# A layer of two mixers on one core: three result buffers for the convolutions, X loaded into the inversion's own tiles, v turned one block later, and two groups of gate columns moved

## The chip, the core and the metric

The kernel runs on one core of a Trainium2 chip. The metric is the device time of one execution in microseconds, and lower is better. The core has a matrix engine (TensorE, in the profile PE, with its weight loads as PEld), VectorE (DVE), ScalarE (ACT), GpSimd (POOL) and SyncE (SP), which here only issues transfers. They run their own instruction streams in order and wait for each other by semaphores. ScalarE and GpSimd issue transfers too.

## The reference

One layer of a diffusion backbone works on 1024 latent tokens and 256 context tokens of width 1024, in float32:

```
h = modulate(rms_norm(x), shift, scale)          # for latent and for context tokens
p = h @ w_in                                     # one projection for both groups of heads
q, k, v = silu(short_conv(p[:, :1536]))          # 4 heads of 128 each
A = tril(k_beta k^T * decay, -1);  T = (I + A)^-1    # one triangular inverse per chunk, head and direction
o_gdn = gated delta rule, both directions        # a scan over chunks; then * silu(z)
o_ret = retention, both directions               # rq and rk with rotary angles; then * silu(rg)
x = x + g1 * (concat(o_gdn, o_ret) @ w_out)
x = x + g2 * swiglu(modulate(rms_norm(x)))
out = rms_norm(x, final_g)
```

The reference scans in chunks of 64 tokens. The kernel uses chunks of 128: 10 in all, 2 of context and 8 latent.

## The kernel before

All of build is written out in Python and scheduled at build time: a planner runs a model of the engines over the program and lays down one fixed order for each engine. Among the instructions that it takes to be ready it picks the one that stands first in the program, so later work fills the holes of earlier work. The order on the chip is then fixed, also where the chip's times differ from the model's.

Memory: pools are stacked from the left or the right side of the on-chip memory. A pool opened after another has been closed lies on the same bytes, and a tile of it waits until the tiles that lay there have been read for the last time. A tag with bufs=n has n slots in turn.

The steps around the change, in the order of the program:

- k blocks, then q blocks. conv_block(b, y, lat) multiplies 128 columns of w_in with all tokens (72 matmuls of three-part float32 products; 48 for q, which needs only latent tokens), copies the two or three chunks from the pc banks of PSUM (2) to u and, scaled, to y with ScalarE (lines 608 and 609), adds four shifted products with VectorE (615), and applies Silu with ScalarE (618). The tiles y come from newy() and have 2 slots, u has 2. Behind each q block qstat turns the q of the block before and sums squares (686, 688), with the pb banks (3).
- token_major(g, ...) multiplies the tokens, tile by tile of 128, with a group of 256 columns: two weight halves, each split in two parts by ScalarE (344) and VectorE or GpSimd (345) into the slots of pool W (2 each; W2 for early groups), then 24 matmuls for a token tile (371 to 373) into a pa bank (3 banks). Groups 0 and 1 are rv, 2 and 3 rk, 4 and 5 rq, 6 and 7 rg (the gate of the retention), 8 and 9 z (the gate of the other group of heads). The finishing step is a Silu (fin_gate, 532) or the rotary turn (fin_rope, 524 to 529, with a scratch tile ra in pool R1). Before the change groups 6 and 7 stand behind the q blocks, groups 8 and 9 behind merge 2, and rk and rq behind the first two steps of the scan.
- solve(b) for the chunks of BATCH 0 (0, 1, 2, 9) and BATCH 1 (3, 8, 4, 7): pre(t) makes the matrices of a chunk. It loads k and q of the chunk (659) and rows of decays (gw, 737), multiplies (729, 734), masks (741, GpSimd), exponentiates (745) and writes U (748) and sp (750). invert(b) sends the diagonal blocks of 32 by 32 to DRAM (yd, 766), loads them back one block to a partition (yr, 768), copies them to L (774, and turned 775), sets X to the identity with GpSimd (771, 772), runs 31 pairs of updates on VectorE (781, 783), and stores X and its turned copy XT (785, 787).
- v blocks. Behind each one its y is turned right away, with ten transposes into three pa banks (871), three copies to vt (873, 2 slots) and three stores issued by ScalarE (874). Then pool CV (y, u, vt) is closed.
- Pools RP (the rope table, loaded by line 887) and GM (matrices U of BATCH 2, t64, xt) open on the bytes of CV. pre(2), merge(0), invert(2), merge(1) and merge(2) follow. A merge loads the inverted blocks (802, 803) and joins them to blocks of 64 and then of 128, with small matmuls (822, 829, 832, 845, 849), copies scaled by -1 on VectorE (825, 846) and copies on ScalarE (835, 838, 851), and stores U (853).
- GM is closed, SC and PK open on its bytes, and the scan over the chunks begins (steps, lines 917 and on).

Of the kernel before, what the change touches and what calls it, by code (L numbers as in the profile page):

```python
# [8 lines left out]
F32 = mybir.dt.float32  # L9
F32R = mybir.dt.float32r  # L10
I32 = mybir.dt.int32
AF = mybir.ActivationFunctionType
ALU = mybir.AluOpType
# [4 lines left out]
P = 128  # L18
# [20 lines left out]
def build(nc, tc, ap, dbg=None, stop=None, marks=None):  # L39
# [19 lines left out]
    def close(p):  # L59
        p_close.pop(id(p)).close()  # L60
# [130 lines left out]
    try:  # L191
# [197 lines left out]
        def token_major(g, tiles, finish, store, pl, q=S):  # L389

            w = [tm_weights(g, kh, pl, q) for kh in range(2)]

            for p in range(0, len(tiles), 2):
                pair = [(t, tm_bank(g)) for t in tiles[p:p + 2]]
                for kh in range(2):
                    for t, o in pair:
                        tm_half(o, w[kh], kh, t)
                for t, o in pair:
                    tm_store(g, t, o, finish, store, pl)
# [118 lines left out]

        def fin_rope(t, o, res):
            cos, sin = rope[:, t, 0:64], rope[:, t, 64:128]  # L520
            ra = R1.tile([P, 2, 2, 64], F32, tag="ra", name="ra")
            o4 = o.rearrange("p (h a d) -> p h a d", a=2, d=64)
            r4 = res.rearrange("p (h a d) -> p h a d", a=2, d=64)
            V.tensor_tensor(ra.rearrange("p h a d -> p (h a) d"), o.rearrange("p (g d) -> p g d", d=64),
                            bc(cos, [P, 4, 64], 1), ALU.mult)
            for a in range(2):
                V.tensor_tensor(r4[:, :, a, :], o4[:, :, 1 - a, :], bc(sin, [P, 2, 64], 1), ALU.mult)
            for a, op in ((0, ALU.subtract), (1, ALU.add)):
                G.tensor_tensor(r4[:, :, a, :], ra[:, :, a, :], r4[:, :, a, :], op)
# [88 lines left out]
            S.activation(y[:, a0:], y[:, a0:], AF.Silu)  # L618

        def newy():  # L620
            return CV.tile([P, NTOK], F32, tag="y", name="y", bufs=2)

        a4, b4, kds4, neG4 = (sm[n].rearrange("p (t d h) -> p t d h", d=2, h=4) for n in ("ab", "beta", "kds", "neG"))

# [39 lines left out]
        V.tensor_scalar(sm["g"], sm["neG"], -1.0, None, ALU.mult)  # L664
        V.tensor_scalar(nkf, nkf, EPS, None, ALU.add)

        lnk = log(GS, nkf, TT * H, "ln").rearrange("p (t h) -> p t h", h=H)
        nG4 = sm["nG"].rearrange("p (t d h) -> p t d h", d=2, h=H)
        V.tensor_scalar(lnk, lnk, 0.5, None, ALU.mult)
        Gr = R2.tile([P, TT, 2, H], F32, tag="Gr", name="Gr", bufs=1)  # L670
# [32 lines left out]
        checkpoint("q")  # L703
        token_major(6, LAT, fin_gate, S, W2, SY)
        qstat(H - 1, qys[H - 1])
        token_major(7, LAT, fin_gate, S, W2, SY)
        checkpoint("rg")
        close(R2)
        close(W2)
# [48 lines left out]
        def invert(b):  # L758

            nc_ = len(BATCH[b])  # L760
            nu = nc_ * H
            nb = 4 * nu
            xd = xds[b] = dr.tile([4 * nb, 1024], F32, tag="xd%d" % b, name="xd%d" % b)
            yr = GI.tile([P, 1024], F32, tag="yr", name="yr", bufs=1)
            for k in range(4):
                SY.dma_start(yd[b][:, k].rearrange("u i j -> i u j"),
                             us[b][q32[k]].rearrange("p e c h j -> p (e c h) j")[:, :, q32[k]])
            SY.dma_start(yr[:2 * nb], yd[b].rearrange("u k i j -> (u k) (i j)"))
            L = GI.tile([P, 1024], F32, tag="L", name="L", bufs=2)
            X = GI.tile([P, 1024], F32, tag="X", name="X", bufs=1)  # L770
            G.memset(X, 0.0)
            G.memset(X[:, 0::33], 1.0)
            m = lambda t: t[:2 * nb].rearrange("p (i j) -> p i j", j=32)
            S.activation(L[:nb], yr[:nb], AF.Copy)
            V.tensor_copy(m(L)[nb:], yr[nb:2 * nb].rearrange("p (i j) -> p j i", j=32))
            for j in range(31):
                n = 31 - j
                tmp = GI.tile([P, 256], F32, tag="tmp", name="tmp", bufs=1)
                t3 = tmp[:2 * nb, :n * (j + 1)].rearrange("p (i c) -> p i c", c=j + 1)
                sh = [2 * nb, n, j + 1]  # L780
                V.tensor_tensor(t3, bc(m(L)[:, j + 1:, j], sh, 2), bc(m(X)[:, j, :j + 1], sh, 1), ALU.mult)
                xs = m(X)[:, j + 1:, :j + 1]
                V.tensor_tensor(xs, xs, t3, ALU.subtract)
            XT = GI.tile([P, 1024], F32, tag="L", name="XT", bufs=2)
            V.tensor_copy(m(XT), X[:2 * nb].rearrange("p (i j) -> p j i", j=32))
            for i, x in enumerate((X[:nb], XT[nb:2 * nb], X[nb:2 * nb], XT[:nb])):
                SY.dma_start(xd[i * nb:(i + 1) * nb], x)
# [19 lines left out]
        def merge(b):  # L807

            uu, ub, t64 = blocks(b)
            nu = len(BATCH[b]) * H  # L810
            q = q32
            u = [x.rearrange("p c h j -> p (c h) j") for x in ub]
            t = t64


            pairs = [(d, p) + ((2 * p, 2 * p + 1) if d == 0 else (2 * p + 1, 2 * p)) for p in range(2) for d in range(2)]
            three = lambda ps, sl, w: ps[sl].rearrange("p (n j) -> p n j", j=w)
            ps1 = bank_b("m1")
            for n in range(nu):
                for d, p, a, bb in pairs:  # L820
                    ca = (a % 2) * 32
                    T.matmul(ps1[q[bb], n * 32:n * 32 + 32], u[d][q[a], n, q[bb]], t[d][q[a], n, ca:ca + 32],
                             start=True, stop=True)
            xt1 = GM.tile([P, 16, 32], F32, tag="xt", name="xt1", bufs=1)
            V.tensor_scalar(xt1.rearrange("p n j -> p (n j)")[:, :nu * 32], ps1[:, :nu * 32], -1.0, None, ALU.mult)
            ps2, ps3 = bank_b("m1"), bank_b("m1")
            for n in range(nu):
                for d, p, a, bb in pairs:
                    T.matmul(ps2[q[a], n * 32:n * 32 + 32], xt1[q[bb], n, :], u[d][q[bb], n, q[bb]],
                             start=True, stop=True)  # L830
                    if p == d:
                        T.matmul(ps3[q[bb], n * 32:n * 32 + 32], u[d][q[bb], n, q[bb]], xt1[q[bb], n, :],
                                 start=True, stop=True)
            for d, p, a, bb in pairs:
                S.activation(u[d][q[a], :, q[bb]], three(ps2[:, :nu * 32], q[a], 32), AF.Copy)
                if p == d:
                    ca = (a % 2) * 32
                    S.activation(t[d][q[bb], :, ca:ca + 32], three(ps3[:, :nu * 32], q[bb], 32), AF.Copy)
            halves = [(0, slice(0, 64), slice(64, 128)), (1, slice(64, 128), slice(0, 64))]
            for n0 in range(0, nu, 8):  # L840
                ps1, ps2 = bank_b("m2"), bank_b("m2")
                xt2 = GM.tile([P, 8, 64], F32, tag="xt", name="xt2", bufs=1)
                for n in range(8):
                    for d, A, B in halves:
                        T.matmul(ps1[B, n * 64:n * 64 + 64], u[d][A, n0 + n, B], t[d][A, n0 + n, :], start=True, stop=True)
                V.tensor_scalar(xt2.rearrange("p n j -> p (n j)"), ps1, -1.0, None, ALU.mult)
                for n in range(8):
                    for d, A, B in halves:
                        T.matmul(ps2[A, n * 64:n * 64 + 64], xt2[B, n, :], u[d][B, n0 + n, B], start=True, stop=True)
                for d, A, B in halves:  # L850
                    S.activation(u[d][A, n0:n0 + 8, B], three(ps2, A, 64), AF.Copy)
            for c, t in enumerate(BATCH[b]):
                S.dma_start(sd[t, :, 1:8:6], uu[:, :, c].rearrange("p e h j -> p e (h j)"))
            checkpoint("mrg%d" % b)
# [5 lines left out]
            invert(b)  # L860
            checkpoint("inv%d" % b)

        solve(0)
        solve(1)
        for h in range(H):
            y = newy()
            conv_block(8 + h, y, False)
            for t0, n in ((0, 2), (2, 4), (6, 4)):
                ps = bank_a("vT")
                for t in range(t0, t0 + n):  # L870
                    T.transpose(ps[:, (t - t0) * P:(t - t0 + 1) * P], y[:, t * P:(t + 1) * P], ident)
                vt = CV.tile([P, 4, P], F32, tag="vt", name="vt", bufs=2)
                S.activation(vt[:, :n], ps[:, :n * P].rearrange("p (t j) -> p t j", j=P), AF.Copy)
                S.dma_start(vd[t0:t0 + n, :, h, :].rearrange("t p j -> p t j"), vt[:, :n])
        close(CV)
        checkpoint("v")
        RP = pool("rp", side="right")
# [13 lines left out]
        merge(2)  # L891


        for g in (8, 9):
            token_major(g, LAT, fin_gate, S, W)
        checkpoint("rgz")
        close(GM)
        close(G2)
# [1 line left out]
        close(GU)  # L900


        SC = pool("sc", bufs=2, side="right")
        PK = pool("pk", side="right")
        dy = dr.tile([LT, P, D], F32, tag="dy", name="dy")
# [247 lines left out]
        close(RT)  # L1153
        close(PK)
        close(SC)
        close(RP)
        close(GS)

# [518 lines left out]
```

## Time and profile before

| | us |
|---|---|
| median of 3 runs (lowest, highest) | 1490.18 (1489.36, 1492.62) |
| time of the profiled execution | 1488.32 |
| its span | 1486.5 |
| granted TensorE clock in it, mean | 0.977 |

The profiled execution's span is 1.8 us shorter than its time, and its time is 1.9 us below the median of the runs. Busy time is given for each engine; "idle before, releaser" tells what ended the idle time in front of an instruction. A line number is that of the kernel before. In a row of the timeline come start, duration, engine, line, operation, output<-inputs, shape and count. The group tm is the work of token_major, b that of conv_block, m that of merge.

### The profile page before, as it was taken

Reading aid. Unit: us, or ns where it says so; the run is one execution under the profiler, and the core shown is the slowest. Engines: PE = TensorE matmul, PEld = TensorE weight load, DVE = VectorE, ACT = ScalarE, POOL = GpSimd, SP = SyncE. Lnnn points to the kernel's source line nnn. Section 1 sums busy time; section 2 is a strip of 40 time slices with the busy share of each in tenths; the row PEclk is TensorE's granted clock in tenths of the full one; section 3 lists DMA queues with packets and bytes.
Section 4 is the critical chain, followed back from the end, with each engine's and each line's share of the span. In section 5 each row is a group of like instructions: output and inputs, shape, how many; then the busy total and the mean of one; then the engine's idle time right before and its main releaser. Section 6 shows DMA issues by size and latency. Waiting matters only on the chain. (4 is left out here: it accounts for less than half of the span.)

```text
span 1486.5 us, 24142 instructions
## 1 busy us (share of the span) xinstructions
PE 1407.3 (95%) x8919; PEld 1207.9 (81%) x8919; DVE 978.0 (66%) x1909; ACT 618.0 (42%) x1342; POOL 579.6 (39%) x493
## 2 busy tenths in 40 slices
PE   7999999996988999899799899999999999999997
PEld 2798888875978999889688688877888888788886
DVE  6568786568666335789777786656555554658577
ACT  5543553866331111346544533323333333444445
POOL 0130010221102344245235588899555553335321
PEclk9999999999889999999899999999999999999999
DMA  9536676478745743996633265765222242685863
GB/s 334 187 105 232 179 235 194 137 221 227 178 130 136 288 165 115 412 367 192 223 124 114 85 210 212 256 236 191 107 107 106 106 145 73 224 293 184 299 220 114
DMA packets 167766, 284.78 MB, mean 192 GB/s; under 512 B 43208, under 2 KB 93592, under 8 KB 163936
## 3 DMA queue, kind: packets, MB, share of 16 engines
q1 hardware_dynamic: 116096, 239.80, 47.6%
q10 hardware_dynamic: 49072, 35.83, 7.8%
q0 software_dynamic: 2480, 7.60, 1.4%
q8 instruction: 70, 1.15, 0.3%
q14 instruction: 48, 0.39, 0.1%
HBM read 201.36 MB, written 81.84 MB: 191 GB/s over the span
## 5 line engine op out<-in xcount | busy, mean ns | idle before, releaser
L371 PE MATMUL tm<-whi,hhi 128*128 128x256 f32 (+1 forms) x704 | 202.7, 293 | 7.5 <-ACT whi L344 3.0
L372 PE MATMUL tm<-wlo,hhi 128*128 128x256 f32 (+1 forms) x704 | 202.8, 290 | 0.7 <-DVE wlo L345 0.7
L373 PE MATMUL tm<-whi,hlo 128*128 128x256 f32 (+1 forms) x704 | 201.4, 290 | 0.0
L371 PEld LDWEIGHTS tm<-whi,hhi 128*128 128x128 f32 x704 | 136.0, 195 | 10.7 <-ACT whi L344 3.2
L372 PEld LDWEIGHTS tm<-wlo,hhi 128*128 128x128 f32 x704 | 137.2, 195 | 2.7 <-DVE wlo L345 1.2
L1366 PE MATMUL ffn<-t,wlo 128*128 128x512 f32 x352 | 137.1, 390 | 1.6 <-DVE wlo L345 1.6
L1364 PE MATMUL ffn<-t,whi 128*128 128x512 f32 x352 | 137.0, 390 | 1.4 <-ACT whi L344 1.4
L373 PEld LDWEIGHTS tm<-whi,hlo 128*128 128x128 f32 x704 | 136.3, 195 | 1.6 <-issue 0.9
L1365 PE MATMUL ffn<-t,whi 128*128 128x512 f32 x352 | 137.0, 389 | 0.0
L344 ACT ACTIVATE whi<-wraw 128x512 fp32r<-128x512 f32 (+2 forms) x98 | 75.2, 771 | 133.1 <-PE ffn L1365 80.2
L344 ACT ACTIVATE whi<-ws 128x512 fp32r<-128x512 f32 x88 | 55.6, 632 | 173.8 <-PE ffn L1365 121.0
L345 DVE TENSOR_TENSOR wlo<-ws,whi 128x512 fp32r<-128x512 f32 x88 | 94.7, 1078 | 48.4 <-ACT whi L344 48.2
L1490 PE MATMUL fo<-whi,ahi 128*128 128x512 f32 x308 | 119.3, 389 | 1.0 <-ACT ahi L344 1.0
L1491 PE MATMUL fo<-wlo,ahi 128*128 128x512 f32 x308 | 119.9, 389 | 0.0
L1492 PE MATMUL fo<-whi,alo 128*128 128x512 f32 x308 | 119.0, 390 | 0.0
L345 DVE TENSOR_TENSOR wlo<-wraw,whi 128x512 fp32r<-128x512 f32 (+2 forms) x92 | 101.5, 1105 | 19.5 <-ACT whi L344 19.2
L1364 PE MATMUL ffn<-b,whi 128*128 128x512 f32 x264 | 103.9, 394 | 5.1 <-ACT whi L344 5.1
L1366 PE MATMUL ffn<-b,wlo 128*128 128x512 f32 x264 | 103.6, 392 | 0.7 <-DVE wlo L345 0.7
L1365 PE MATMUL ffn<-b,whi 128*128 128x512 f32 x264 | 103.4, 392 | 0.0
L615 DVE SCALAR_TENSOR_TENSOR y<-u,cw,y 128x1022 f32<-128x1022 f32 (+3 forms) x80 | 81.9, 1040 | 19.7 <-ACT y L609 19.2
L607 PE MATMUL b<-hhi,wlo 128*128 128x512 f32 (+1 forms) x256 | 94.7, 370 | 0.0
L606 PE MATMUL b<-hlo,whi 128*128 128x512 f32 (+1 forms) x256 | 94.3, 368 | 0.0
(451 smaller groups left out, 3440.1 us busy)
## 6 DMA issues: line engine op xcount, KB each, us to landing
adaw<-ada SPq DMA_DIRECT2D x48, 512.0 KB, 4.4
pk<-sd SPq DMA_DIRECT2D x16, 1536.0 KB, 15.0
wraw<-wfi SPq DMA_DIRECT2D x44, 512.0 KB, 4.2
ar<-ad SPq DMA_DIRECT2D x33, 512.0 KB, 4.2
w<-wfo SPq DMA_DIRECT2D x22, 512.0 KB, 4.3
wd<-tw SPq DMA_DIRECT2D x11, 1024.0 KB, 4.9
ad<-act SPq DMA_DIRECT2D x20, 512.0 KB, 3.1
raw<-wd SPq DMA_DIRECT2D x20, 512.0 KB, 4.7
```

Source lines behind the costliest of these rows:

```text
L344: S.activation(hi, raw, AF.Copy)
L345: e.tensor_tensor(lo, raw, hi.bitcast(F32), ALU.subtract)
L371: T.matmul(o, hhi[:, k, tsl], whi[:, k % 4, :], start=(k == 0), stop=False)
L372: T.matmul(o, hhi[:, k, tsl], wlo[:, k % 4, :], start=False, stop=False)
L373: T.matmul(o, hlo[:, k, tsl], whi[:, k % 4, :], start=False, stop=(k == KT - 1))
L607: T.matmul(o, wlo[:, k, :], hh, start=False, stop=(k == KT - 1))
L1364: T.matmul(o, whi[:, k, :], xhi(xn, slice(0, 4), k), start=(first and k == 0), stop=False, **kw)
L1365: T.matmul(o, whi[:, k, :], xlo(xn, slice(0, 4), k), start=False, stop=False, **kw)
L1366: T.matmul(o, wlo[:, k, :], xhi(xn, slice(0, 4), k), start=False, stop=(k == 3), **kw)
L1490: T.matmul(po[g][i], ahi[:, ts], whi, start=(j == 0 and not kw), stop=False, **kw)
L1491: T.matmul(po[g][i], ahi[:, ts], wlo, start=False, stop=False, **kw)
L1492: T.matmul(po[g][i], alo[:, ts], whi, start=False, stop=(j == FH - 1), **kw)
```

## The change

- y has 3 slots in place of 2 (newy).
- token_major(7), the second half of rg, moves from behind the q blocks to behind the last v block. token_major(8), the first half of z, moves from behind merge(2) to the same place. Both now use pool W.
- v is turned by a function vturn, called for block h-1 behind block h, and for the last block behind groups 7 and 8. vt shrinks to two tiles of 128, so a block is copied and stored in five pieces (was three).
- In invert the loaded rows go straight to X[nb:2nb] and L[:nb]; yr and ScalarE's copy go. X has 2 slots (was 1) and is set to the identity by VectorE, behind the turned copy that reads it. XT is L itself, no longer a second slot.
- In merge the two copies scaled by -1 move from VectorE to ScalarE.
- The scratch ra of fin_rope moves from R1 to a pool RA that opens when GM has been closed, ahead of SC. The scratch of log moves from GS to R2.

```diff
-            ra = R1.tile([P, 2, 2, 64], F32, tag="ra", name="ra")
+            ra = RA.tile([P, 2, 2, 64], F32, tag="ra", name="ra")
...
-            return CV.tile([P, NTOK], F32, tag="y", name="y", bufs=2)
+            return CV.tile([P, NTOK], F32, tag="y", name="y", bufs=3)
...
-        lnk = log(GS, nkf, TT * H, "ln").rearrange("p (t h) -> p t h", h=H)
+        lnk = log(R2, nkf, TT * H, "ln").rearrange("p (t h) -> p t h", h=H)
...
         token_major(6, LAT, fin_gate, S, W2, SY)
         qstat(H - 1, qys[H - 1])
-        token_major(7, LAT, fin_gate, S, W2, SY)
...
-            yr = GI.tile([P, 1024], F32, tag="yr", name="yr", bufs=1)
+            L = GI.tile([P, 1024], F32, tag="L", name="L", bufs=2)
+            X = GI.tile([P, 1024], F32, tag="X", name="X", bufs=2)
...
-            SY.dma_start(yr[:2 * nb], yd[b].rearrange("u k i j -> (u k) (i j)"))
-            L = GI.tile([P, 1024], F32, tag="L", name="L", bufs=2)
-            X = GI.tile([P, 1024], F32, tag="X", name="X", bufs=1)
-            G.memset(X, 0.0)
-            G.memset(X[:, 0::33], 1.0)
+            rows = yd[b].rearrange("u k i j -> (u k) (i j)")
+            SY.dma_start(X[nb:2 * nb], rows[nb:])
+            SY.dma_start(L[:nb], rows[:nb])
...
-            S.activation(L[:nb], yr[:nb], AF.Copy)
-            V.tensor_copy(m(L)[nb:], yr[nb:2 * nb].rearrange("p (i j) -> p j i", j=32))
+            V.tensor_copy(m(L)[nb:], X[nb:2 * nb].rearrange("p (i j) -> p j i", j=32))
+            V.memset(X, 0.0)
+            V.memset(X[:, 0::33], 1.0)
...
-            XT = GI.tile([P, 1024], F32, tag="L", name="XT", bufs=2)
+            XT = L
...
-            V.tensor_scalar(xt1.rearrange("p n j -> p (n j)")[:, :nu * 32], ps1[:, :nu * 32], -1.0, None, ALU.mult)
+            S.activation(xt1.rearrange("p n j -> p (n j)")[:, :nu * 32], ps1[:, :nu * 32], AF.Copy, scale=-1.0)
...
-                V.tensor_scalar(xt2.rearrange("p n j -> p (n j)"), ps1, -1.0, None, ALU.mult)
+                S.activation(xt2.rearrange("p n j -> p (n j)"), ps1, AF.Copy, scale=-1.0)
...
+        def vturn(h, y):
...
+                for t in range(t0, t0 + n, 2):
+                    vt = CV.tile([P, 2, P], F32, tag="vt", name="vt", bufs=2)
+                    S.activation(vt, ps[:, (t - t0) * P:(t - t0 + 2) * P].rearrange("p (t j) -> p t j", j=P), AF.Copy)
+                    S.dma_start(vd[t:t + 2, :, h, :].rearrange("t p j -> p t j"), vt)
...
+        vys = []
         for h in range(H):
-            y = newy()
-            conv_block(8 + h, y, False)
...
+            vys.append(newy())
+            conv_block(8 + h, vys[h], False)
+            if h:
+                vturn(h - 1, vys[h - 1])
+        token_major(7, LAT, fin_gate, S, W)
+        token_major(8, LAT, fin_gate, S, W)
+        vturn(H - 1, vys[H - 1])
         close(CV)
...
-        for g in (8, 9):
-            token_major(g, LAT, fin_gate, S, W)
+        token_major(9, LAT, fin_gate, S, W)
...
+        RA = pool("ra", bufs=2, side="right")
         SC = pool("sc", bufs=2, side="right")
...
         close(SC)
+        close(RA)
```

More of the change, by code (lines that the diff above doesn't have):

```diff
@@ L861, in solve @@
             checkpoint("inv%d" % b)
-        solve(0)
-        solve(1)
-        for h in range(H):
-            y = newy()
-            conv_block(8 + h, y, False)
+        def vturn(h, y):
             for t0, n in ((0, 2), (2, 4), (6, 4)):
@@ L871, in build @@
                     T.transpose(ps[:, (t - t0) * P:(t - t0 + 1) * P], y[:, t * P:(t + 1) * P], ident)
-                vt = CV.tile([P, 4, P], F32, tag="vt", name="vt", bufs=2)
-                S.activation(vt[:, :n], ps[:, :n * P].rearrange("p (t j) -> p t j", j=P), AF.Copy)
-                S.dma_start(vd[t0:t0 + n, :, h, :].rearrange("t p j -> p t j"), vt[:, :n])
+                for t in range(t0, t0 + n, 2):
+                    vt = CV.tile([P, 2, P], F32, tag="vt", name="vt", bufs=2)
+                    S.activation(vt, ps[:, (t - t0) * P:(t - t0 + 2) * P].rearrange("p (t j) -> p t j", j=P), AF.Copy)
+                    S.dma_start(vd[t:t + 2, :, h, :].rearrange("t p j -> p t j"), vt)
+        solve(0)
+        solve(1)
+        vys = []
+        for h in range(H):
+            vys.append(newy())
[5 more added lines that the diff above has]
+        vturn(H - 1, vys[H - 1])
         close(CV)
```

## The prediction

> **What bounds the kernel now.** I read the page first (engines, slices, granted clock), then busy time by stage, then what TensorE waits for, then the rows around the edited lines.
>
> ```profile
> span 1486.5 us, 24142 instructions
> PE 1407.3 (95%) x8919; PEld 1207.9 (81%) x8919; DVE 978.0 (66%) x1909; ACT 618.0 (42%) x1342; POOL 579.6 (39%) x493
> PEclk9999999999889999999899999999999999999999
> ```
>
> TensorE is busy for 95% of the span, so what it idles or runs slowly is what can be won. Each digit of the clock is a fortieth of the span, 37 us: two 8 stand side by side from 372 to 446 us. By stage (columns: length, busy time and count of PE, PEld, DVE, ACT, POOL, granted clock, DMA share, GB/s):
>
> ```profile
> 236.00:262.00 26.00, 26.00 (x207) 23.90 (x205) 14.25 (x41) 9.77 (x32) 1.11 (x2) 1.00 0.66 195
> 290.00:371.00 81.00, 64.62 (x389) 56.48 (x387) 62.53 (x96) 55.10 (x120) 15.34 (x17) 0.95 0.79 228
> 371.00:398.00 27.00, 26.60 (x202) 26.40 (x202) 17.07 (x45) 10.27 (x19) 5.32 (x5) 0.89 0.62 163
> 398.00:439.00 41.00, 36.72 (x640) 34.62 (x640) 29.74 (x77) 10.42 (x19) 2.71 (x3) 0.88 0.52 131
> 439.00:500.00 61.00, 53.46 (x959) 50.28 (x960) 33.13 (x86) 13.76 (x24) 16.75 (x30) 0.92 0.68 202
> 500.00:583.00 83.00, 83.00 (x712) 83.00 (x712) 33.62 (x110) 9.79 (x19) 36.17 (x74) 1.00 0.41 150
> ```
>
> TensorE's largest waits from 236 to 500 (total, times, longest):
>
> ```profile
> PE vT L871 <- ACT y L618: 11.2, 3, 8.7
> PE kq L734 <- issue: 5.2, 2, 2.6
> ```
>
> From 290 to 500 TensorE idles for 16.4 + 0.4 + 4.3 + 7.5 = 28.6 us, 11.2 of them ahead of the turns of v. Behind a stall it also runs slowly (last columns: clock, DMA, GB/s):
>
> ```profile
> 372.00:376.00 4.00, 4.00 (x20) 0.50 0.42 123
> 444.00:448.00 4.00, 4.00 (x21) 0.50 1.10 202
> ```
>
> The missing clock times the length of each stage gives 4.1 + 3.0 + 4.9 + 4.9 = 17 us; part of it falls into idle time, so I count 14. Some 42 us are thus lost from 290 to 500, and no more can be won. From 500 to 583 TensorE is full at full clock, so I pass a shift made ahead of 500 on to the end one to one.
>
> **The change, part by part.** *The third buffer of y, and group 7 taken out of the q stage.*
>
> ```profile
> 230.76 0.60 ACT L608 ACTIVATE u<-b 128x512 f32<-128x512 f32 x1 [3.34 <-PE b L607]
> 260.09 1.26 ACT L609 ACTIVATE y<-b,cw 128x512 f32<-128x512 f32 x2
> L371 PE MATMUL tm<-whi,hhi x63: 279/281/365, 236.1 to 261.5; 128*128 128x256 f32 x63
> 262.66 0.39 PE L605 MATMUL b<-hhi,whi 128*128 128x512 f32 x1
> ```
>
> The copy of q2 to y comes 29 us after that to u: it waits for a slot of y. The last q block cannot start until 262.66, and group 7 (64 triples, 63 of them in this row) fills TensorE meanwhile: 26.00 busy of 26.00. With three slots the q block runs at 236 and group 7 later; TensorE does the same work in another order, so I price this at 0. What covers it: the q and v blocks themselves. If that fails, nothing fills in any more; the two kq waits of 2.6 us are the nearest rows, so 0 to +6, and no gain of its own. The solves start some 22 us sooner, and VectorE, busy for only 14 of 26 us here and for 62.5 of 81 in the v stage, gets its work spread out.
>
> *v turned one block later.*
>
> ```profile
> 369.76 1.27 ACT L618 ACTIVATE y<-y 128x1280 f32<-128x1280 f32 x1 [0.49 <-DVE y L615]
> 371.08 2.40 PE L871 MATMUL vT<-ident,y 128*128 128x128 f32 x10 [8.73 <-ACT y L618]
> ```
>
> TensorE stands before the last turn because VectorE finishes the convolution late, with an inversion interleaved. In the new order another block, and at the end groups 7 and 8, lie between, so the 11.2 us and the half clock behind 371 (2 us in 372:376, 3 in all) go. Late next: the first tiles of group 7, since the turns of v2 hold all three pa banks until ScalarE has copied them, now in five pieces of two tiles through two slots.
>
> ```profile
> DMA to landing us min/median/max: 1.8/4.1/4.7
>   DMA sd<-vt: 5.2, 3
> ```
>
> (Both of tile vt: time to landing, and ScalarE's idle time until a slot's store has landed.) A piece through a slot costs a copy, an issue and 1.8 us at the least; three waits for a block where there was one. I take 4 us of TensorE at the start of group 7 (0 to 8); what is queued behind on ScalarE are the conv copies, which have the slack of two pc banks.
>
> *Groups 7 and 8 ahead of the last turn.* A group is 192 matmuls; the step between starts is
>
> ```profile
> 424.44 0.28 PE L373 MATMUL tm<-whi,hlo 128*128 128x256 f32 x1
> 427.50 0.28 PE L372 MATMUL tm<-wlo,hhi 128*128 128x256 f32 x1
> 399.00 0.22 PE L822 MATMUL m<-t,U 32*32 32x32 f32 x2 [1.32 <-DMA t<-xd]
> 441.85 1.01 PE L371 MATMUL tm<-whi,hhi 128*128 128x256 f32 x3 [3.03 <-ACT whi L344]
> ```
>
> 3.06 us over 26 steps = 0.118, so a group is 22.6 us. Between groups the two weight slots turn over: the two lower rows are the boundaries 8 to 9 and 9 to rk. The new boundary 7 to 8 costs 1.3 to 6 us (3.03 and as much again at half clock); I take 4.5.
>
> [...]
>
> *Sum up to the end of group 8.* Before, that point is 397.5, with 16.8 idle and, of the 7.1 of clock, about 4 outside it lost since 290: 21. After, lost: the kq waits 5.2 and 1.6 of clock, 4 at the start of group 7, 4.5 at the boundary: 15.3. Gain **6 us**: group 8 ends near 391.5, and the last turn of v comes behind it, as the program orders it.
>
> *Behind the last turn: pre(2), inversion 2, merge 2.* Matrices 2 and t64 lie where CV's y was, so this chain begins at the last turn (373.5 before, 391.5 after). The rope's scratch ra, until now in R1, is put where the merges' xt lies: no rope before merge 2 has read it.
>
> ```profile
> L524 DVE TENSOR_TENSOR ra<-tm,rope x10: 406/418/425, 451.1 to 492.6; 128x256 f32<-128x256 f32 x10
> L371 PE MATMUL tm<-whi,hhi x93: 276/281/579, 441.8 to 497.2; 128*128 128x256 f32 x93
> 497.63 1.15 PE L849 MATMUL m<-U,xt 64*64 64x64 f32 x32
> ```
>
> Before, 93 triples of rk (32.8 us) filled TensorE during merges 1 and 2. After, only three tiles fit (three pa banks, 8.5 us), and 24.3 us move behind merge 2. The length of the chain, from these rows:
>
> ```profile
> 377.88 0.33 SPq L887 DMA_DIRECT2D rope<-rope  x1
> 378.31 0.38 SPq L737 DMA_DIRECT2D gw<-grow_d  x1
> 385.12 0.69 DVE L748 TENSOR_TENSOR U<-kk,gw 128x512 f32<-128x512 f32 x1 [3.56 <-ACT gw L745]
> 311.79 1.60 SPq L766 DMA_DIRECT2D yd<-U  x3
> 329.77 1.39 DVE L775 COPY L<-yr 64x1024 f32<-64x1024 f32 x1
> 395.56 0.21 DVE L781 TENSOR_TENSOR tmp<-L,X 128x31 f32<-128x31 f32 x1 [5.13 <-POOL X L772]
> 428.44 1.06 DVE L785 COPY XT<-X 128x1024 f32<-128x1024 f32 x1
> 433.87 0.20 DVE L781 TENSOR_TENSOR tmp<-L,X 64x31 f32<-64x31 f32 x1 [2.52 <-POOL X L772]
> 469.43 0.78 SPq L787 DMA_DIRECT2D xd<-X  x2
> 480.71 0.24 PE L822 MATMUL m<-t,U 32*32 32x32 f32 x2 [2.29 <-DMA t<-xd]
> 433.00:470.00 37.00, 22.28 (x63) 0.91 0.57 151
> ```
>
> (The last row is VectorE on tile X alone.) Last turn to U: 385.8 - 373.5 = 12.3. U to the loaded block: 18.0 in batch 0 (311.8 to 329.8), with other loads in the queue; 9 if only issues and landings count; I take 10, the queue being emptier. The turned copy and two memsets now on VectorE: 2. The updates: 22.3 busy, 35.5 with rope and weights between; those are gone, so 24. Stores and reloads 469.4 to 480.7: 11.3. Merge 2: 18 (480.7 to 498.8) with matmuls of rk between; without them I take 13. Sum **73 us**; ends 66 (with 9, 1, 22.3 and 10) and 97 (with 18, 2, 35.5 and 18). TensorE's work within it: group 9 22.6, merges about 25 (101 less 22.6, 32.8, 12 idle and 9 of clock), rk 8.5: 56. It idles for 17.
>
> Before, 398 to 499 held the same work and 24.3 us more of rk: 101. After: 73 + 24.3 + 1.7 (half clock at the restart) = 99. Gain **2 us**.
>
> *The small ones together.* Direct loads into L and X, X double and zeroed on VectorE, XT in L: the waits for X ahead of L781, 5.13 and 2.52, go; 5.13 is inversion 1's, hidden by groups 7 and 8, and 2.52 lies ahead of my 24. xt on ScalarE in place of VectorE: a copy for a copy, in a merge with slack. lnk in R2: nothing. Each is priced at nothing; uncovered, the two waits would be a gain of 7.6. If inversions 0 and 1 were still running at 391, their 33 us each (395.6 to 428.4, with two weights between) would lengthen the chain; starting 22 us sooner, they should end near 380.
>
> Sum: 6 + 2 = 8 us. The profiled execution took 1488.3 us (span 1486.5): 1480.3. The median of the three runs stands 1.9 above it: **1482 us**.
>
> **The rivals.** (1) *The last turn slips ahead of group 8.* If the planner sees a hole in TensorE at the boundary 7 to 8, the ten turns go there, and the chain starts 22.6 us sooner, over 56 + 22.6 = 79 us of work, longer than the chain. Of the 17 idle us some 4 stay, for the next boundary of groups. Gain 6 + 2 + 13 = 21, time 1469. For it: merge 0's pair at 399.00 stands exactly at such a boundary. Against: that pair is ahead of the group in the program, the turn is behind it.
>
> (2) *Slower: rk waits for merge 2.* The chain grows as its pieces did before (18, 35.5, 18): 97 us, 22 more than 101 - 24.3 - 1.7 = 75 allows. The rope table's load waits for the last vt store, and gw behind it on SP, which gives it 4 more us easily. With the 6 it turns slower from a chain of 81 us; at 97 the time is 1506, typically (88) 1497. For it: slow pieces are what the trace shows. Against: their neighbours on VectorE are gone.
>
> (3) *No change.* The q and v blocks wait uncovered for y, u or pb, as the kq rows do, for 6 to 10 us, and the 8 are gone: 1490.
>
> **How the numbers follow.** Forecast 0.42, rival 1 0.25, rival 2 0.20, rival 3 0.13. The forecast's own range, chain 68 to 80: 1477 to 1489. 0.2% (3 us) is about what tells a change from none here. Faster: 0.33 of the forecast and 0.25 = 0.58. Same: 0.06 and 0.08 of rival 3 = 0.14. Slower: 0.03, 0.20, 0.05 = 0.28. The range leaves out the far ends of rivals 1 and 2: 1465 to 1500.
>
> **What would show it.** Right: no group of rows tm between the q blocks at 236 to 262; vT no longer waits for y; a gap of TensorE of some 17 us behind group 9; the first ra row only behind the last L849 row. Rival 1: vT between the matmuls of group 7 or 8. Rival 2: from last vT to the last merge over 81 us. The prediction fails if ra lands on free memory, or if inversion 1 still runs when pre(2) is done.

## The result and the profile after

The changed kernel takes **1505.8 us** (median of 4 runs, 1503.1 to 1510.1); the kernel before, run beside it, 1489.8 us. The ratio is 1.0109, 95% interval 1.0080 to 1.0139: **16 us slower**, where 1482 was predicted. The profiled execution took 1506.0 us, its span 1504.2. All medians here and below are of fast runs; one run, of e9, was slow (2839.7 us) and is left out.

The page of the changed kernel, the same three lines as before:

```profile
span 1504.2 us, 24164 instructions
PE 1399.9 (93%) x8919; PEld 1202.0 (80%) x8919; DVE 976.6 (65%) x1907; ACT 618.5 (41%) x1353; POOL 577.8 (38%) x487
PEclk9999999999995899999899999999999999999999
```

As many matmuls, TensorE 93% busy instead of 95%, and in the slice from 451 to 489 us a 5, where the kernel before has no digit under 8. The stages (columns as in the prediction):

```profile
236.00:262.00 26.00, 16.38 (x97) 12.49 (x95) 15.93 (x40) 8.39 (x28) 2.40 (x1) 0.87 0.59 176
262.00:351.00 89.00, 79.47 (x472) 68.80 (x470) 61.20 (x92) 66.93 (x184) 21.11 (x21) 0.98 0.71 204
351.00:400.00 49.00, 48.70 (x399) 48.65 (x400) 40.48 (x93) 13.70 (x28) 0.00 (x0) 0.97 0.47 135
400.00:450.00 50.00, 42.04 (x687) 39.78 (x687) 26.56 (x66) 17.78 (x33) 3.34 (x3) 0.97 0.72 169
450.00:485.00 35.00, 21.32 (x712) 19.30 (x713) 12.46 (x39) 13.08 (x25) 0.84 (x3) 0.56 0.70 224
485.00:610.00 125.00, 115.12 (x972) 114.73 (x972) 48.16 (x152) 13.00 (x24) 52.35 (x106) 0.96 0.41 150
```

Two stages that were full are not any more: the q stage (16.38 busy of 26) and the tm stretch behind the merges (115 of 125). In 450 to 485 TensorE is busy for 21 of 35 us, at a clock of 0.56. The stages of v and of groups 7 and 8, 262 to 400, are in order. Whom TensorE waits for, from 200 us to the first ffn matmul (total, times, longest; rows in order of time):

```profile
PE gr L504 <- DVE acc L499: 8.7, 1, 8.7
...
PE tm L371 <- ACT vt L870: 3.3, 2, 2.8
PE vT L867 <- ACT y L618: 2.1, 1, 2.1
...
PE m L844 <- ACT t L837: 5.2, 5, 1.8
PE m L828 <- ACT xt L824: 4.2, 2, 2.5
PE m L848 <- ACT xt L845: 4.1, 4, 1.4
...
PE kS L939 <- DVE S L967: 9.8, 1, 9.8
...
PE ro L1114 <- DMA vg<-rd: 11.9, 1, 11.9
```

The waits for y ahead of the turns are down from 11.2 to 2.1 us. New are 8.7 us in the q stage, some 14 in the merges' round trips to ScalarE, 9.8 at the scan's second step, and 11.9 late in the retention. Where the kernels stand at four points, by the end or start of TensorE's rows in each trace (us; e2 and e4 are explained below):

| | before | changed | e2 | e4 |
|---|---|---|---|---|
| last turn of v ends | 373.5 | 400.5 | 401.5 | 374.7 |
| last merge ends | 498.8 | 483.3 | 497.4 | 489.8 |
| tm matmuls left then | 588 | 792 | 557 | 792 |
| last tm ends | 582.9 | 608.4 | 579.3 | 603.9 |
| first ffn matmul | 838.8 | 857.3 | 831.5 | 854.6 |

The changed kernel is 15.5 us ahead when the merges end, and 25.5 behind when tm ends.

### The profile page after: what moved, and what is told of

Its sections match the earlier page's. It is cut to its first block, busy times and chain, and to the rows that moved or that the text cites. A ratio compares the mean times of both kernels' runs of the same rounds, so it can differ in the third digit from the quotient of the medians.

```text
span 1504.2 us, 24164 instructions
## 1 busy us (share of the span) xinstructions
PE 1399.9 (93%) x8919; PEld 1202.0 (80%) x8919; DVE 976.6 (65%) x1907; ACT 618.5 (41%) x1353; POOL 577.8 (38%) x487
## 4 chain that ended last, share of the span: by engine, by line
PE 52%; DMA 8%; DVE 8%; POOL 6%; issue 3%; ACT 2%; SPq 2%; ACTq 0%; POOLq 0%; DVEq 0%
PE ffn L1376 6%; PE ffn L1374 6%; PE ffn L1375 6%; PE fo L1500 5%; PE fo L1502 5%; PE fo L1501 5%; PE tm L373 3%; PE tm L371 3%; PE tm L372 3%; PE op L1235 2%; PE op L1233 2%; PE op L1234 2%; DMA gw<-grow_d 2%; DMA wd<-tw 2%; DMA sd<-U 1%
## 5 line engine op out<-in xcount | busy, mean ns | idle before, releaser
L371 PE MATMUL tm<-whi,hhi 128*128 128x256 f32 (+1 forms) x704 | 199.0, 287 | 6.3 <-ACT vt L870 3.3
L373 PE MATMUL tm<-whi,hlo 128*128 128x256 f32 (+1 forms) x704 | 198.1, 285 | 0.0
L372 PEld LDWEIGHTS tm<-wlo,hhi 128*128 128x128 f32 x704 | 133.9, 190 | 2.6 <-DVE wlo L345 1.2
L605 PE MATMUL b<-hhi,whi 128*128 128x512 f32 (+1 forms) x256 | 95.0, 371 | 2.0 <-ACT y L609 2.0
## 6 DMA issues: line engine op xcount, KB each, us to landing
pk<-sd SPq DMA_DIRECT2D x16, 1536.0 KB, 11.9
```

Of the source, the lines that this page charges most:

```text
L371: T.matmul(o, hhi[:, k, tsl], whi[:, k % 4, :], start=(k == 0), stop=False)
L372: T.matmul(o, hhi[:, k, tsl], wlo[:, k % 4, :], start=False, stop=False)
L373: T.matmul(o, hlo[:, k, tsl], whi[:, k % 4, :], start=False, stop=(k == KT - 1))
```

## The experiments

The theory (A in the expectations): the loss consists of holes that each belong to one part, the late place of ra above all. Its rival: the chain behind the last turn bounds, whatever lies beside it.

**e1, the q stage's hole.**

```diff
 conv_block(h, y, True)
-if h < 2:
-    ada_rest(5, h)
 ...
 if h:
     qstat(h - 1, qys[h - 1])
+if h < 2:
+    ada_rest(5, h)
```

> The changed kernel with one reordering: in the q stage the turns of the q block before (qstat) stand ahead of the second pair of coefficient rows (ada_rest(5, .)) instead of behind them. Theory A (the loss is made of holes, each belonging to one part): TensorE stands 8.7 us at 248 because the coefficient matmul L504, which waits for its weights, stands ahead of the turns that free the y slot the next v block needs; with the turns first the hole goes and the kernel is 8 to 13 us faster than the changed one, about 1495. Rival (the chain behind the last turn of v is all that bounds): the v blocks start earlier but wait for VectorE or a y slot later, and the time stays within 3 us of 1506.

Measured: 1498.5 us (10 runs, 1488 to 1501), ratio to the kernel before 1.0049 (1.0027 to 1.0071): 7 us faster than the changed kernel. Its q stage has one wait of 2.5 us left, and the last turn ends at 393.5 instead of 400.5. So the hole was real, and its cause the order on TensorE; the gain is just under the 8 to 13 us that theory A expected.

**e2, ra early; e3, both; e4, ra late in the kernel before.** e2 in the changed kernel:

```diff
-ra = RA.tile([P, 2, 2, 64], F32, tag="ra", name="ra")
+ra = RP.tile([P, 2, 2, 64], F32, tag="ra", name="ra", bufs=2)
 ...
-RA = pool("ra", bufs=2, side="right")
```

RP, the rope's pool, opens behind the last turn of v. e3 is e1 and e2 together. e4 is the kernel before with the changed kernel's two ra lines.

> The changed kernel with ra taken from the rope's pool, which opens behind the last turn of v, instead of a pool opened behind merge 2: the rope of rk can run during the merges again. Theory A: the merges' 13.7 us of holes and half clock from 450 to 485 are filled, and so is the 9.8 us hole at 493, where the scan's second step stands with no rk beside it: 10 to 25 us faster than the changed kernel, 1481 to 1496, with well over 80 tm matmul triples of rk before the last merge. Rival (the merge chain bounds, whatever fills it): the chain from the last turn to the last merge grows by as much as rk brings forward, gain under 4 us.

> Both edits of e1 and e2 in the changed kernel. Theory A: the two gains add, 18 to 35 us faster than the changed kernel, 1471 to 1488, so at or below the kernel before. Rival (one bound behind both): no better than the better of e1 and e2 by more than 3 us.

> The kernel before with nothing changed but ra's place: from a pool that opens behind merge 2. Theory A: taking rk out of the merges alone costs 12 to 25 us, 1502 to 1515, with the tm matmuls of rk limited to three tiles before the last merge. The prediction's reckoning (the chain shortens once rk's rows leave VectorE, which pays for the 24.3 us of rk that move behind it): within 7 us of 1490.

Measured: e2 **1481.7 us**, ratio 0.9943 (0.9921 to 0.9965); e3 1480.1, ratio 0.9928 (0.9908 to 0.9948); e4 **1504.8**, ratio 1.0107 (1.0054 to 1.0159). ra's place alone decides the sign. It costs 24 us in the changed kernel and 15.5 in the kernel before (1489.3 in these runs), about as much as the whole change loses; the rest of the change gains 8. e4's four runs scatter (1499.5 to 1515.1), so by its interval its cost lies anywhere from 8 to 24 us; that it is less than in the changed kernel is not clear from the times. The stretch of the merges, and the first rope, changed kernel first and then e2:

```profile
483.45 0.42 DVE L524 TENSOR_TENSOR ra<-tm,rope 128x256 f32<-128x256 f32 x1 [21.51 <-PE m L848]
```

```profile
441.22 0.42 DVE L524 TENSOR_TENSOR ra<-tm,rope 128x256 f32<-128x256 f32 x1 [0.35 <-PE tm L373]
419.00:497.40 78.40, 71.02 (x1502) 67.17 (x1503) 41.34 (x108) 27.28 (x48) 20.24 (x37) 0.96 0.70 191
L371 PE MATMUL tm<-whi,hhi x81: 274/281/582, 445.8 to 496.0; 128*128 128x256 f32 x81
```

In the changed kernel the first rope waits for the last merge, 21.51 us with VectorE idle. In e2 it runs at 441; by the last merge 103 triples of rk are done, 81 of them from 445.8 on (third row), against 24 in the changed kernel, and TensorE is busy for 71 of 78 us at 0.96. e2's merges end 14 us later with 235 fewer tm matmuls to go (792 - 557; 27.7 us at the prediction's 0.118). e3's time lies in theory A's wide range too, but it is not the sum (7 and 24 us off 1505.8 would be 1475), and the rival, at most 3 us better than e2, fits: its last turn is 7 us sooner than e2's and its tm ends 6.9 sooner (572.4), but its first ffn matmul only 2.0 sooner (829.5), and the time 1.6, within the scatter. The scan and the retention give it back; which wait there takes it was not traced to one row. e1's 7 us are so a gain only while ra is late.

**e5, the rope table's load moved.** In the changed kernel the last piece of vt leaves its bytes so late (its store, issued at 408.16, lands 1.8 us later) that the table's load, and the gw load behind it on SP, go out 10 us behind the last turn (410.06 and 410.51, against 400.5). The edit, and the same in e3 as e6:

```diff
-SY.dma_start(rope, ap["rope"])
 invert(2)
+with tc.issue_after(loaded[0]):    # behind inversion 2's load of L
+    SY.dma_start(rope, ap["rope"])
```

> The changed kernel with the load of the rope table moved behind inversion 2's loads on SP. In the changed kernel the last gw load (410.51) stands on SP behind the rope load (410.06), which waits until the last of the five vt pieces has left the bytes that the table takes; from the last turn to inversion 2's stores 22.6 us pass, against 12.3 before. Theory A: with gw ahead that piece falls to about 13, the chain from the last turn to the last merge from 83 to about 74, and the time by 6 to 9 us to 1497 to 1500. Rival: the first two merges, which end at 472.4 just as merge 2 becomes ready, are a second chain of the same length; merge 2 only waits for them instead, and the time stays within 3 us of 1506.

> e3 (turns first in the q stage, ra from the rope's pool) with the rope load moved as in e5. Theory A: with rk free to fill the merges the chain behind the last turn no longer bounds, so it is worth less than in e5: 0 to 4 us, 1476 to 1480. Rival: rk waits for the rope table and loses its place in the merges, 3 to 10 us slower than e3, 1483 to 1490.

Measured: e5 1507.9 us, ratio 1.0119 (1.0089 to 1.0149), no gain; e6 1479.3, ratio 0.9930 (0.9907 to 0.9953), equal to e3 within the scatter. The timeline of e5:

```profile
416.67 2.65 SPq L768 DMA_DIRECT2D yd<-U  x4
454.40 1.51 SPq L788 DMA_DIRECT2D xd<-X  x2
483.71 1.97 PE L850 MATMUL m<-U,xt 64*64 64x64 f32 x32 [0.75 <-ACT xt L847]
```

The chain did get shorter: inversion 2's blocks are stored at 416.67 and ready at 454.40, 6.5 us sooner than in the changed kernel (423.13 and 460.90). The last merge still ends 2.4 us later, behind merges 0 and 1, whose own round trips end at 474.8. This is the rival of e5: there are two chains of nearly one length, and theory A's chain of about 74 did not come, for from the last turn (399.8) to the last merge (485.7) it is 85.9 us.

**e7, the last turn between groups 7 and 8, ra late.**

```diff
 token_major(7, LAT, fin_gate, S, W)
+vturn(H - 1, vys[H - 1])
 token_major(8, LAT, fin_gate, S, W)
-vturn(H - 1, vys[H - 1])
```

> The changed kernel with the last turn of v ahead of group 8 instead of behind it; ra stays late. Theory A (what is missing behind the last turn is work to lie beside the chain): 22.6 us of group 8 now lie beside it, the last merge ends some 15 us sooner, and the time falls by 12 to 18 us to 1488 to 1494. Rival (the holes sit in merges 1 and 2, behind the last group in any case, and only rk can fill them): the holes of 450 to 485 stay, gain under 5 us.

Measured: 1499.3 us, ratio 1.0067 (1.0042 to 1.0091), 6.4 faster than the changed kernel: more than the rival allowed and half of what theory A expected. The last turn ends 21.6 us sooner (378.9), the last merge 10.3 (473.0), and the merges run at

```profile
403.70:473.00 69.30, 59.14 (x1386) 55.54 (x1385) 37.81 (x97) 25.82 (x48) 0.95 (x1) 0.90 0.71 189
```

59 us busy of 69 at 0.90, against 46.7 of 65.6 at 0.75 in the changed kernel's merges (417.7 to 483.3). Group matmuls fill as rk does, but 24 us of rk still lie behind.

**e8, group 7 back in the q stage, in e2.**

```diff
 qstat(H - 1, qys[H - 1])
+token_major(7, LAT, fin_gate, S, W2, SY)
 ...
-token_major(7, LAT, fin_gate, S, W)
 token_major(8, LAT, fin_gate, S, W)
```

> e2 (ra from the rope's pool) with group 7 back in the q stage, where the kernel before had it. Theory A: group 7 covers the 8.7 us hole at 248, the q stage gains as in e1, but as in e3 most of it is given back in the scan: 1477 to 1482. Rival (moving the group behind the last v block was worth something by itself, as cover for the last turns of v): TensorE waits ahead of the turns again, 1484 to 1490.

Measured: 1486.2 us (10 runs, 1479 to 1489), ratio 0.9970 (0.9949 to 0.9992), 4.5 slower than e2 by the medians, with overlapping runs. The time is in the rival's range, but the wait that the rival named does not show: no wait ahead of the turns of v is over 0.4 us, and the longest, 5.4 us, is ahead of turns of q (L686, until ScalarE's L688). From 236 us to the last turn TensorE idles for 12.7 us, less than e2's 19.3. tm ends 2.0 us later than in e2 (581.3) and the first ffn matmul comes 5.4 later (836.9), so the loss shows mostly behind tm; its cause is open.

**e9, a fifth vg buffer, and e10, one scan step ahead of rk, in the changed kernel.** e9 changes the 4 in each `load(RT, ..., "vg", 4, ...)` to 5, e10 `NS0 = 2` to 1.

> The changed kernel with five buffers of vg instead of four in the retention. Every kernel with ra late shows a hole of about 12 us near the end of the retention (11.95 at 744.56 in the changed kernel), in which the last vg load has come late. Theory A (the hole is a cost of its own, through the buffers of vg): with a fifth buffer the load goes out earlier, the hole goes, and the time falls by 7 to 12 us to 1494 to 1499. Rival (it only takes the place of other waits: from the end of tm to the first ffn matmul the kernel before needs 255.9 us without the hole, the changed one 248.9 with it): within 3 us of 1506.

> The changed kernel with one step of the scan instead of two ahead of the groups rk and rq (NS0 = 1). Theory A: the 9.8 us hole at 493 (kS of the second step waits for VectorE's copy of S, which waits for a store of merge 2) goes, since rk lies ahead of that step: 5 to 10 us faster, 1496 to 1501. Rival (the scan, a serial chain, ends later by what it starts later): within 4 us of 1506, with the tm matmuls ending sooner and the retention later.

Measured: e9 1504.2 us (three runs), ratio 1.0106 (1.0074 to 1.0137); e10 1504.6, ratio 1.0093 (1.0068 to 1.0119). e9's wait for vg is gone and its retention's last matmul 10.4 us sooner (738.2 against 748.6), but the first ffn matmul only 1.6 (855.7): three waits for yt and ylo ahead of the projection (6.1 us), and a mean clock of 0.97 there, take its place. The largest single wait after the merges cost nothing. e10 did not do what it was meant to. Its rows:

```profile
502.36 0.69 DVE L967 COPY S<-up 128x512 f32<-128x512 f32 x1 [9.10 <-DMA sd<-U]
503.93 0.55 PE L371 MATMUL tm<-whi,hhi 128*128 128x256 f32 x1 [6.09 <-DVE res L527]
```

The copy of S that waits for merge 2's store belongs to the first step; VectorE stands at it as before, and rk now waits for VectorE. tm does end 9.2 us sooner (599.2), but the first ffn matmul comes no sooner (858.0), and the time is in the rival's range.

**e11, v turned at once, in e2.**

```diff
 conv_block(8 + h, vys[h], False)
-if h:
-    vturn(h - 1, vys[h - 1])
+vturn(h, vys[h])
 ...
-vturn(H - 1, vys[H - 1])
 close(CV)
```

> e2 (ra from the rope's pool) with each block of v turned right behind its own convolution, as in the kernel before; groups 7 and 8 stay in program order behind the v blocks. Theory A (the prediction's step): TensorE waits for y ahead of the turns again, 8 to 12 us in all, of which the move had won about 6: 5 to 9 us slower than e2, 1487 to 1491. Rival (groups 7 and 8 are ready and fill the wait of the last turn, so only the order on paper changes): within 3 us of 1482.

Measured: 1492.0 us (10 runs, 1490 to 1499), ratio 1.0031 (1.0013 to 1.0048): 10 us slower than e2. The profiled run is the slowest of the ten (1499.2). Its waits from 262 to 400:

```profile
PE kq L733 <- issue: 8.7, 2, 7.8
PE b L605 <- ACT y L609: 6.4, 3, 4.1
PE vT L867 <- ACT y L618: 4.4, 2, 4.0
```

In that run TensorE idles for 21.5 us from 262 to 400, in e2 for 10.4. The edit also puts the last turn ahead of groups 7 and 8, and in e12 below its place ahead of group 8 goes with a loss of 5 us. So the later turn is worth some 5 to 10 us, about what the prediction gave it or somewhat more; part of the price shows at the next convolution and at kq instead of at vT.

**e12, everything together**: e3 with e7's and e9's edits.

> Everything that helped, together: e3 (turns first in the q stage, ra from the rope's pool) with the last turn of v ahead of group 8 (e7) and five buffers of vg (e9). Theory A: with rk free to fill, the place of the last turn is worth 0 to 4 us and the fifth buffer nothing, as e3 shows no vg hole: 1476 to 1480. Rival (the stages behind the merges bound the kernel, whatever is won ahead of them): equal to e3 within 1 us, 1479 to 1481.

Measured: 1485.4 us (12 runs, 1478 to 1489), ratio 0.9965 (0.9950 to 0.9980): 5 us slower than e3, which neither expected. The last turn ends 24 us sooner (370.0 against 394.5) and the last merge at the same time (485.5, 485.1). 660 tm matmuls are then left, against e3's 623. With rk free to fill, the last turn's place wins nothing. In the profiled runs, 3.7 us apart, tm ends 10.2 us later than in e3 (582.6), the first ffn matmul only 1.6 (831.2); what makes up the 5 us is open.

**e13, merge 2's store on SP, in the changed kernel.**

```diff
-S.dma_start(sd[t, :, 1:8:6], uu[:, :, c]...)
+(SY if b == 2 else S).dma_start(sd[t, :, 1:8:6], uu[:, :, c]...)
```

> The changed kernel with the stores of merge 2's matrices issued by SP instead of ScalarE, so that on SP two of the large pk loads (1.5 MB each) stand behind them. In the changed kernel the store is issued at 484.6 and lands 16.6 us later, behind pk loads, and VectorE's copy of S at 501.84 waits for it (8.59 us), with TensorE idle for 9.81 us. Theory A (this hole is the part of ra's price that the kernel before does not pay, 24 against 15.5 us): the store lands by about 495, the hole shrinks to 2 to 6 us, and the time falls by 4 to 8 us to 1498 to 1502. Rival (the DMA queues are full until 502 in any order, and what does not wait for the store waits for a pk load): within 2 us of 1506.

Measured: 1501.4 us, ratio 1.0074 (1.0052 to 1.0095), 4.3 faster than the changed kernel. The row of S, in the changed kernel and in e13:

```profile
501.84 0.69 DVE L967 COPY S<-up 128x512 f32<-128x512 f32 x1 [8.59 <-DMA sd<-U]
```

```profile
497.81 0.69 DVE L967 COPY S<-up 128x512 f32<-128x512 f32 x1 [4.49 <-DMA sd<-U]
```

S is copied 4 us sooner, and TensorE's 9.8 us hole becomes two of 3.1 and 0.9: 5.8 won there, 4.3 in the time. This hole is a cost, and, if the two prices of ra (24 and 15.5 us) differ, as the ends of tm suggest (29 against 21 us later), the likely reason why the kernel before pays less, since in e4 TensorE does not idle between its last merge and the end of tm (489.8 to 603.9).

The best version is e6, 1479.3, with e3 (1480.1) equal to it: 0.7% under the kernel before.

## Why the prediction was wrong, by its steps

*The third buffer, priced at 0.* The step held, its cover did not. The q block moved up as said (the last q block's matmuls start at 228.4), and no tm of group 7 is left there. But the next block, v0, then needs the slot of the first q block:

```profile
256.83 1.87 PE L504 MATMUL gr<-acc,ones 128*1 128x512 f32 x2 [8.72 <-DVE acc L499]
258.62 1.60 PE L686 MATMUL qt<-ident,y 128*128 128x128 f32 x8
...
262.14 0.39 PE L605 MATMUL b<-hhi,whi 128*128 128x256 f32 x1
```

```profile
261.41 1.25 ACT L609 ACTIVATE y<-b,cw 128x512 f32<-128x512 f32 x2
```

The slot comes free by the turns qt, and these stand on TensorE behind L504, whose sum acc waits on VectorE for loaded weights (adaw):

```profile
252.28 1.54 DVE L499 SCALAR_TENSOR_TENSOR acc<-adaw,csl,acc 128x512 f32<-128x512 f32 x2 [1.96 <-DMA adaw<-ada]
255.14 1.54 DVE L499 SCALAR_TENSOR_TENSOR acc<-adaw,csl,acc 128x512 f32<-128x512 f32 x2 [1.33 <-DMA adaw<-ada]
```

The copies of y follow at 261.41, v0 at 262.14. So v0 starts when in the kernel before the last q block did (262.66): one block was won, and the hole opened ahead of the next. In the kernel before the same matmul was as late (the last of its rows starts at 257.9), with group 7 beside it:

```profile
L504 PE MATMUL gr<-acc,ones x4: 590/590/591, 245.0 to 257.9; 128*1 128x512 f32 x4
```

"The q and v blocks themselves" could not cover, being what waited. Bound named 0 to +6, measured 7 at the last turn (e1).

*v turned later: right.* The waits for y fell from 11.2 to 2.1, the new wait at group 7 was 2.8 where I took 4, and the boundary between groups 7 and 8, at 4.5, showed no hole. By e11 the step is worth some 5 to 10 us.

*Group 8 ends near 391.5.* It ended at 399.4, the last turn behind it at 400.5: 9 late, most of it the q stage; with that mended, e1's last turn ends at 393.5.

*The chain of 73 us.* It took 83 (400.5 to 483.3). The changed kernel's rows, by which the pieces can be checked:

```profile
410.06 0.35 SPq L896 DMA_DIRECT2D rope<-rope  x1
410.51 1.02 SPq L736 DMA_DIRECT2D gw<-grow_d  x1
...
423.13 2.60 SPq L766 DMA_DIRECT2D yd<-U  x4
```

```profile
434.42 1.05 DVE L772 COPY L<-X 32x1024 f32<-32x1024 f32 x1 [6.54 <-DMA X<-yd]
460.91 1.03 DVE L784 COPY L<-X 64x1024 f32<-64x1024 f32 x1
```

```profile
472.38 1.07 PE L821 MATMUL m<-t,U 32*32 32x32 f32 x64
...
481.36 1.97 PE L848 MATMUL m<-U,xt 64*64 64x64 f32 x32 [0.75 <-ACT xt L845]
```

Last turn to the stores of U 22.6 (12.3 taken), to the loaded block 11.3 (10), copy and memsets 2.4 (2), updates 24.1 (24), stores and reloads 11.5 (11.3), merge 2 10.9 (13). One term of the chain was mis-sized, by 10 us, the way from the last turn to U: vt in five pieces through two slots, the rope table behind them, gw behind that. Rival 2 named this queue and gave it 4. But e5, in which this way takes 16.9 us, is no faster: merges 0 and 1, with nothing of rk beside them, end at the same time, and the prediction had no term for that second chain.

*rk behind merge 2.* **This is the step that failed.** The amount was right: 204 more tm matmuls lie behind the last merge, 24.1 us at 0.118, against 24.3. What it cost was not. I charged the move against a chain shortened by the same amount and kept a gain of 2; e2 shows a cost of 24 and e4 of 15.5. The merges did end earlier, by 14 us against e2, too little to pay for 27.7 us of tm matmuls that e2 no longer has to do. The half clock I took as 1.7 us at the restart (the kernel before has one of that price at 310 to 318, by means of 0.74 and 0.84 in two stretches of 4 us) runs through the merges (0.56 from 450 to 485). And the scan's start, for which I had no term, stands 9.8 us until merge 2's store has landed.

*The copies xt, priced at nothing for their slack.* TensorE waits 8.3 us for them in the changed kernel's merges (4.2 + 4.1, above), 3.7 in e4, where VectorE makes them, and in e2 not at all. So the slack was rk's, and went with it; no run moves these copies alone.

The sum: 9 at the last turn, 10 in the chain, 15 from the last merge to the end of tm (125.1 against 84.1 + 24.3 + 1.7 = 110.1), less 8 behind it, where before needs 903.6 us to the end and the changed kernel 895.8: 26, the distance from 1480.3 to 1506.0. The 8 and part of the 15 are one thing: between the last merge and the end of tm lie 171 matmuls other than tm in the changed kernel and 131 before, some 7 us of TensorE, all of the scan, which are then done. The sum says where the time went, not what each place costs: the 9 at the last turn stand in e2 too, and mending them there, in e3, won 1.6. e2 came to the forecast's 1482, but not by its terms: its last turn ends 10 us later than the sum had it, and its tm at 579.3, where 582.9 - 8 gives 574.9. Of the signs named, "the first ra row only behind the last merge" held, and so did rival 2's (83 against the 81 at which it turns slower); its time, 1506, was met too, but by luck: it gave that time for a chain of 97 us, for one of 83 its reckoning gives about 1492.

## What to carry to other kernels

Before a scratch tile is moved to memory that comes free later, list the work that cannot run until then, and ask what else can lie beside the waits that it filled; if nothing can, charge its whole length, less only what a trace shows the stretch to shrink by. When a filler is taken out of a stage, look for the next thing on the same queue that it had been hiding, since a block that itself waits covers nothing. And price a hole by an experiment: of two of about 10 us here, one gave 4 when it shrank to 4, and the other nothing clear of the scatter when it was gone.

## What the hardware showed unexpectedly

The clock in the changed kernel's merges, in stretches of 4 us:

```profile
452.00:456.00 4.00, 1.50 (x130) 1.25 (x120) 3.66 (x11) 0.88 (x2) 0.00 (x0) 0.78 0.83 310
456.00:460.00 4.00, 1.43 (x115) 1.16 (x103) 3.59 (x13) 0.60 (x2) 0.00 (x0) 0.50 0.05 12
...
464.00:468.00 4.00, 3.25 (x60) 3.06 (x58) 0.00 (x0) 0.96 (x2) 0.00 (x0) 0.50 0.55 90
...
484.00:488.00 4.00, 3.93 (x30) 3.74 (x29) 2.24 (x11) 1.77 (x3) 3.02 (x6) 0.88 1.04 391
```

It falls inside a gap of 2.49 us that ends at 454.75 (the mean of 0.78 puts the fall near 454.2) and stays at 0.50 to 484. No later gap in that time is over 1.92 us, and TensorE is busy for 3.25 of 4 us at 464. TensorE works without a gap from 481.36, and the mean of 0.88 in the stretch from 484 puts the return near 485. The half clock among many short gaps lasted longer than the one at a single long gap: some 31 us here, some 7 around the gap of 8.72 us that ends at 256.83 (0.86, 0.50 and 0.79 in the stretches of 4 us from 250 to 262).

Merge 2's store, issued by ScalarE at 485.0, took 16.6 us to land, against a median of 4.3 for that line, with 1.5 MB pk loads under way from SP. With merge 2's stores issued by SP ahead of two of these loads, in e13, the slowest of the line took 12.2.

Two gaps of the merges have no releaser in the profile: 2.76 us to 434.10 and 1.92 to 458.56, each in the middle of a row of 32x32 matmuls. In each stretch the queue that the page calls "instruction" moved one packet of 16 KB (431 to 433 us, then 456 to 458):

```profile
q8 instruction: 1, 0.02, 3.6%
q8 instruction: 1, 0.02, 3.5%
```

Whether the matmuls waited for what that queue moved, no run tests.
